# A fourth buffer for the weight sums of a fast matrix product, with tables loaded per mixer to make the room

## Chip, cores and metric

One core of a Trainium2 chip. The metric is device microseconds from the kernel's start to its end. TensorE (PE in the profile) multiplies, VectorE (DVE) and ScalarE (ACT) do the elementwise work, GpSimd (POOL) only issues transfers that add to what lies in the destination, SyncE (SP) issues most loads.

## The reference

An encoder of two layers on 512 tokens and 16 prepended ones, width 1024, all in float32:

```python
for l in range(DEPTH):                       # DEPTH = 2
    h = h + 0.5 * swiglu(rmsnorm(h, g[l, 0]), gate[l, 0], up[l, 0], down[l, 0])   # width 2816
    h = h + mixer(rmsnorm(h, g[l, 1]), ...)  # gated linear attention + softmax attention, merged by gates
    h = h + 0.5 * swiglu(rmsnorm(h, g[l, 2]), gate[l, 1], up[l, 1], down[l, 1])
return rmsnorm(h, final_norm)[:, N_META:]

def swiglu(x, w_gate, w_up, w_down):
    return (jax.nn.silu(x @ w_gate) * (x @ w_up)) @ w_down
```

In the softmax attention the queries and keys are turned by rotary angles, with a table of cosines and one of sines over the tokens. In the gated linear attention the decay comes from a low-rank product, `lr @ gla_w2 + gla_b2`.

## The kernel before

Activations lie with the channels on the 128 partitions and the 528 tokens along the free axis. Every float32 product is made from three products of rounded parts: a weight block of 128 x 1024 is split into a high part (`whi`, a cast on ACT, L287) and a low part (`wlo`, a subtraction on DVE, L288), and TensorE multiplies high by high, high by low and low by high.

In a feed-forward block the gate and up products go by a scheme with seven instead of eight products of half-size blocks (Strassen's, in Winograd's form), per pair of column groups. There are eleven pairs, and four more such sets of products for most of the down product. The seven products of a pair are named "1" to "7". Products "1", "2" and "4" use blocks of the weights as they are (`DIRECT`); "7", "3", "6" and "5" use sums of blocks, which are made while they are loaded:

- third and fourth sum (`s3`, `s4`, products "7" and "3") live in the pool of long sums, tag `wsa`;
- second and first sum (`s2`, `s1`, products "6" and "5") live in the pool of short sums, tag `wsb`.

Both pools are opened in `block_pools` with three buffers each; blocks used as they are have three buffers of their own (`wraw`), and four buffers hold high and low parts. For pairs 0 and 1 `s3` and `s4` begin as a negated copy of a block on ACT (L203), to which POOL's queue adds by a transfer (L208). From pair 2 on `s3` is loaded by SP (L198) and DVE subtracts a block from it (L253); `s4` is a subtraction on DVE (L256). `s1` is always a load by SP and an addition by POOL's queue. `begin_sums` asks for the sums of a pair when the block of its product "1" is fetched, nine loads ahead of use.

In the very first block the order of the products is P0 "1" "2", P1 "1" "2", P0 "4", P1 "4", P0 "6" "5" "7" "3", P1 "6" "5", P2 "1", P1 "7", P2 "2", P1 "3", P2 "6" "5" and so on: one product (a tile) is 24 matmuls. The order within each engine's queue is set by a planner when the program is built: it takes an instruction when its inputs and its buffer are there by its own reckoning, in the order of the program where several are. On the chip each queue then runs in that fixed order.

Rotary tables, identity and other constants lie in one tile `ct`, loaded by `load_constants` behind the first silu of the first block (L395 to L398); only 128 columns of it come earlier, by SP. The low-rank weights (`w2t`) have one tile for the whole program. A mixer opens its own pools on the left of the memory, where the sums' pools and the pool `c` of the feed-forward block lay; the operands (`x` or `xc`) lie on the right.

Of the kernel before, what the change touches and what calls it, by code (L numbers as in the profile page):

```python
# [10 lines left out]
F32 = mybir.dt.float32  # L11
F32R = mybir.dt.float32r
# [5 lines left out]
P = 128  # L18
D = 1024
KC = D // P  # L20
SEQ = 512
META = 16
T = SEQ + META
# [137 lines left out]
NPAR = G_FIN + KC  # L161


C_COS, C_SIN = 0, T
C_ID = 2 * T
C_O1024, C_O128, C_B64 = C_ID + P, C_ID + 2 * P, C_ID + 3 * P
C_DIAG = C_ID + 4 * P
NCONST = C_DIAG + P


class Weights:
# [157 lines left out]
def build(tc, ctx, xt, wts, win, par, w2, const, umask, out):  # L329
# [32 lines left out]
    def nm(p):  # L362
        count[0] += 1
        return f"{p}{count[0]}"
# [3 lines left out]
    def slot(tag, dtype=F32, n=None):  # L368
        return slots[tag].tile([P, T], dtype, tag=tag, name=nm(tag))[:, : n or live[0]]
# [24 lines left out]
    S.dma_start(pt, par)  # L394
    def load_constants():  # L395
        S.dma_start(ct[:, :C_O1024], const[:, :C_O1024])
        S.dma_start(ct[:, C_O1024 + P :], const[:, C_O1024 + P :])
        S.dma_start(mask, umask)  # L398

    eps = one.tile([P, 1], F32, name="eps")  # L400
    V.memset(eps, EPS)
    cos, sin = ct[:, C_COS : C_COS + T], ct[:, C_SIN : C_SIN + T]
    ident = ct[:, C_ID : C_ID + P]
    o1024, o128 = ct[:, C_O1024 : C_O1024 + P], ct[:, C_O128 : C_O128 + P]
    b64, diag2 = ct[:, C_B64 : C_B64 + P], ct[:, C_DIAG : C_DIAG + P]
# [384 lines left out]
    def gla_pair(l, p, lr, w2t, sr, qa, ka, va, n_out):  # L790
# [17 lines left out]
        for d in range(2):  # L808
            z = pair()
            for i, hs in enumerate(halves):  # L810
                c0 = p * 256 + d * P
                TE.matmul(z[:, i, :HF], w2t[:, c0 : c0 + P], lr[:, hs], start=True, stop=True)
            a, g, c, ct_ = slot("t"), slot("t"), slot("t"), slot("t")

            S.activation(v2(a), z[:, :, :HF], AF.Abs)
            S.activation(a, a, AF.Exp, scale=-1.0)
            S.activation(a, a, AF.Ln, bias=1.0)
            V.scalar_tensor_tensor(v2(g), z[:, :, :HF], 0.0, v2(a), ALU.min, ALU.subtract)
            ones = ct[:, C_COS + SEQ : C_COS + SEQ + 1]
            for bs in [b[1] for b in blocks] + [MB]:  # L820
                n = bs.stop - bs.start
                V.tensor_tensor_scan(c[:, bs], ones.broadcast_to([P, n]), g[:, bs], 0.0, ALU.mult, ALU.add)
            mid = blk(c)[:, :, 63:64].broadcast_to([P, NB, P])
            tot = blk(c)[:, :, 127:128].broadcast_to([P, NB, P])
            mm_ = c[:, T - 1 : T].broadcast_to([P, META])
            r16 = 1.0 / 16.0
            src = c
            if d == 1:
                V.tensor_tensor(g, c, g, ALU.subtract)
                src = g  # L830

            def to_end():
                V.tensor_tensor(blk(ct_), blk(src), tot, ALU.subtract)
                V.tensor_tensor(ct_[:, MB], src[:, MB], mm_, ALU.subtract)


            ke = slot("p")
            if d == 0:
                to_end()
                S.activation(ke, ct_, AF.Exp, scale=-r16)  # L840
            else:
                S.activation(ke, g, AF.Exp, scale=r16)
            V.tensor_tensor(ke, ka, ke, ALU.mult)
# [12 lines left out]
            V.tensor_tensor(blk(a), blk(src), mid, ALU.subtract)  # L856
            V.tensor_tensor(a[:, MB], src[:, MB], mm_, ALU.subtract)
            qp, kp = slot("p"), slot("p")
            S.activation(g, a, AF.Exp, scale=-r16)
            S.activation(a, a, AF.Exp, scale=r16)  # L860
            if d == 0:
                S.activation(c, c, AF.Exp, scale=r16)
                ein, eq, ek = c, a, g
            else:
                S.activation(ct_, ct_, AF.Exp, scale=-r16)
                ein, eq, ek = ct_, g, a
            V.tensor_tensor(qp[:, :n_out], qa, eq[:, :n_out], ALU.mult)
            V.tensor_tensor(kp, ka, ek, ALU.mult)
            if qin is None:
                qin = [slot("p"), slot("p")]  # L870
            e0 = 127 if d == 0 else 0
            for hh in range(2):
                rows = slice(hh * HD, (hh + 1) * HD)
                to = slice(d * HD, (d + 1) * HD)
                V.tensor_tensor(qin[hh][to, :n_out], qa[rows], ein[rows, :n_out], ALU.mult)
                V.tensor_copy(dec[to, hh, :], blk(ein)[rows, :, e0])
            prods.append((qp, kp))
# [70 lines left out]

    swap = [(i + 16) % 32 for i in range(32)]

    def rope(src, gc):

        n = src.shape[-1]
        sh = slot("t", n=n)
        V.stream_shuffle(sh, src, swap)
        V.scalar_tensor_tensor(src, src, col(gc), cos[:, :n], ALU.mult, ALU.mult)
        V.scalar_tensor_tensor(sh, sh, col(gc + 1), sin[:, :n], ALU.mult, ALU.mult)
        V.tensor_tensor(src, src, sh, ALU.add)

    def attention(l, x, rs, n_out):  # L960

        meta = n_out == T
        kt = project(x, rs, "i")
# [1 line left out]
        sq, y = slot("t"), slot("t")  # L965
        S.activation(sq, kt, AF.Square)
        rsqrt_of(means(b64, sq), y, True)
        rope(kt, G_KN + 2 * l)
        V.scalar_tensor_tensor(kt, kt, -0.5, y, ALU.mult, ALU.mult)

        vpp = pair()
# [24 lines left out]
        def prologue(g):  # L996
# [28 lines left out]
                    V.tensor_scalar(r, r, -0.0625, None, ALU.mult)  # L1025
            for c in range(2):
                q = qt[2 * g + c]
                rope(q, G_QN + 2 * l)
                if meta:
                    V.tensor_tensor(q[:, MB], q[:, MB], rq[:, 16 + c * META : 16 + (c + 1) * META], ALU.mult)  # L1030
                bt[2 * g + c] = slot("e", n=n_out)
                for e in range(2):
                    a, b = slice(e * HD, (e + 1) * HD), slice((1 - e) * HD, (2 - e) * HD)
                    qq = slot("p", F32R, n_out)
                    S.copy(qq[a], q[a])
                    V.tensor_tensor(qq[b], q[a], qq[a].bitcast(F32), ALU.subtract)
                    if meta:
                        V.tensor_copy(qm[:, 2 * c + e], qq[:, MB].bitcast(F32))
                    qs.append(qq)
# [82 lines left out]
        norm.pools = open_pools("right", **{"x": dict(x=16), "xc": dict(xc=8)}[kind])  # L1122

    def block_pools():
        pools = open_pools("left", wsa=3, wsb=3)
        W.long, W.short = pools["wsa"], pools["wsb"]
        return pools

    def mixer(l, norm, done, following):

        x, n_out = norm.x, T if l < DEPTH - 1 else SEQ
        pools = open_pools("left", e=8, i=5, p=7, q=6, k=5, lr=1)
        banks = open_pools("left", psum=("mm", "sm"), mm=2, sm=2)
        w2r, w2t, w2l = slots["p"].tile([P, T], F32, tag="p", name=nm("w2")), one.tile([P, 512], F32R, tag="w2", name=nm("w2")), slot("t")
        S.dma_start(w2r[:, :512], w2[l])
        w2r, w2l = w2r[:, :512], w2l[:, :512]
        S.copy(w2t, w2r)
        V.tensor_tensor(w2l, w2r, w2t.bitcast(F32), ALU.subtract)
# [10 lines left out]
            sr.append(r)  # L1149
        table("natural_log_exp_and_others")  # L1150
        lr = slot("lr", F32R)
        S.copy(lr[96:P], cos[96:P, SEQ : SEQ + 1].broadcast_to([32, T]))

        ps, both = Acc("sm"), slot("p", F32R)[:, : KC * HD].rearrange("p (k s m) -> p k s m", k=KC, s=2)
        for i, (copy, t) in enumerate(zip((S.copy, V.tensor_copy), W.row("w_in", KC))):
# [24 lines left out]
                gates.extend(project(x, None, both[:, i], n=n_out) for i in range(2))  # L1180

        gate_pairs(EARLY // 2)
        bt = attention(l, x, rs, n_out)
        gate_pairs(KC - EARLY // 2)
        live[0] = n_out
        a = [split(t, "x") for t in sr]
# [116 lines left out]
def constants():  # L1303
    f32 = np.float32
    inv = (f32(10000.0) ** (-np.arange(0, HD // 2, 2, dtype=f32) / f32(HD // 2))).astype(f32)
    row = np.repeat(np.arange(SEQ // 64), 64).astype(f32)
    colm = np.tile(np.arange(64), SEQ // 64).astype(f32)
    ang = np.zeros((HD, T), f32)
    sign = np.ones((HD, 1), f32)
    for d in range(HD):  # L1310
        ang[d, :SEQ] = (row if d < 32 else colm) * inv[d % 16]
        sign[d] = -1.0 if d % 32 < 16 else 1.0
    c = np.zeros((P, NCONST), f32)
    c[:, C_COS : C_COS + T] = np.tile(np.cos(ang), (2, 1))
    c[:, C_SIN : C_SIN + T] = np.tile(np.sin(ang) * sign, (2, 1))
    c[:, C_ID : C_ID + P] = np.eye(P)
    c[:, C_O1024 : C_O1024 + P] = 1.0 / D
    c[:, C_O128 : C_O128 + P] = 1.0 / P
    c[:, C_B64 : C_B64 + P] = np.kron(np.eye(2), np.ones((HD, HD))) / HD
    c[:, C_DIAG : C_DIAG + P] = 1.0 + np.eye(P)  # L1320
    return c, (np.arange(P)[:, None] > np.arange(P)[None, :]).astype(np.uint32)
# [49 lines left out]
```

## Time and profile before

| | us |
|---|---|
| median of 3 runs (lowest, highest) | 2209.68 (2209.25, 2211.64) |
| profiled execution, device time | 2211.05 |
| its span, first to last instruction | 2209.2 |
| PE, DVE, ACT, POOL busy | 2162.4, 1785.4, 1214.1, 101.8 |
| granted TensorE clock, mean | 0.997 |

In the rows below, L198 is a line of the kernel; `w<-win` is what is written and what it is made from, by the program's names with numbers left out; xN is a count. A row of the timeline is start, duration, engine, line, operation, and in brackets the idle time of the engine just before it and what ended that. A row of the stage table has, per engine, the busy time and the number of instructions, then the granted clock, the mean busy share of the 16 DMA engines and what they moved. The spans of DMA issues (SPq, POOLq) are those of the issuing queue; the transfer itself takes longer.

### The profile page before, as it was taken

The numbers are of one execution on the slowest core, as the hardware profiler recorded it, in microseconds if no ns is written. First come the engines' busy times: TensorE is split into PE (matmuls) and PEld (weight loads), VectorE is DVE, ScalarE is ACT, GpSimd is POOL, SyncE is SP. The second block draws the span as 40 slices with busy tenths as digits, with TensorE's granted clock in tenths as the row PEclk, the third lists the DMA queues.
The fourth block names the chain that finished last, engine by engine and source line by source line (L and its number), as shares of the span: only waits on it lengthen the run. The fifth ranks groups of instructions, "written<-read, shape, count | busy, mean of one in ns | idle before, by whom it ended". The sixth has DMA issues, their size and how long they took to land.

```text
span 2209.2 us, 40079 instructions
## 1 busy us (share of the span) xinstructions
PE 2162.4 (98%) x16506; PEld 2070.2 (94%) x16506; DVE 1785.4 (81%) x2703; ACT 1214.1 (55%) x1779; POOL 101.8 (5%) x120
## 2 busy tenths in 40 slices
PE   7999999999999999999999999999999999999998
PEld 6999999989999999999999999999788888999997
DVE  7897978486886689889789979775879767997987
ACT  7544545344785555454575445453457836554543
POOL 1000000000000001000010000000000001000100
PEclk9999999999999999999999999999999999999999
DMA  9775753212113468666567757432121145776752
GB/s 268 189 204 160 191 152 106 82 49 68 49 39 122 114 167 205 190 182 187 162 163 186 207 164 191 143 110 77 49 84 51 42 133 152 198 202 181 189 165 67
DMA packets 87463, 311.41 MB, mean 141 GB/s; under 512 B 9712, under 2 KB 12144, under 8 KB 87280
## 3 DMA queue, kind: packets, MB, share of 16 engines
q1 hardware_dynamic: 68624, 245.53, 32.9%
q0 software_dynamic: 16704, 60.82, 15.8%
q8 instruction: 130, 2.13, 0.4%
q10 hardware_dynamic: 1952, 2.50, 0.4%
q14 instruction: 53, 0.43, 0.1%
HBM read 289.94 MB, written 2.10 MB: 132 GB/s over the span
## 4 chain that ended last, share of the span: by engine, by line
PE 81%; DVE 11%; ACT 4%; issue 2%; DMA 2%; SPq 0%; DVEq 0%; ACTq 0%
PE ss L598 37%; PE mm L465 13%; PE ss L712 11%; PE ss L465 10%; PE sm L465 2%; DVE wlo L288 2%; DMA w<-win 2%; PE sm L1074 1%; PE ss L1049 1%; DVE g L678 1%; ACT whi L287 1%; PE sm L1090 1%; DVE h L720 1%; PE ss L471 1%; PE sm L1091 1%
## 5 line engine op out<-in xcount | busy, mean ns | idle before, releaser
L598 PE MATMUL ss<-xc,whi 128*128 128x264 f32 (+1 forms) x4928 | 907.2, 285 | 15.5 <-ACT whi L287 7.4
L598 PEld LDWEIGHTS ss<-xc,whi 128*128 128x128 f32 x4928 | 767.2, 189 | 20.4 <-ACT c L602 8.4
L598 PE MATMUL ss<-xc,wlo 128*128 128x264 f32 (+1 forms) x2464 | 702.5, 285 | 8.8 <-DVE wlo L288 8.8
L598 PEld LDWEIGHTS ss<-xc,wlo 128*128 128x128 f32 x2464 | 466.5, 189 | 11.1 <-DVE wlo L288 10.9
L288 DVE TENSOR_TENSOR wlo<-w,whi 128x1024 fp32r<-128x1024 f32 (+1 forms) x337 | 408.1, 1217 | 63.4 <-ACT whi L287 63.2
L287 ACT CAST whi<-w 128x1024 fp32r<-128x1024 f32 (+1 forms) x337 | 350.0, 1050 | 163.3 <-PE ss L598 80.5
L465 PE MATMUL mm<-x,whi 128*128 128x264 f32 (+1 forms) x1712 | 384.6, 315 | 0.0
L465 PEld LDWEIGHTS mm<-x,whi 128*128 128x128 f32 x1712 | 278.3, 188 | 16.5 <-issue 1.0
L465 PE MATMUL mm<-x,wlo 128*128 128x264 f32 (+1 forms) x856 | 266.0, 315 | 0.0
L712 PE MATMUL ss<-g,whi 128*128 128x264 f32 (+1 forms) x1280 | 237.4, 284 | 0.0
L287 ACT CAST whi<-raw 128x1024 fp32r<-128x1024 f32 x126 | 132.3, 1050 | 163.4 <-PE mm L465 102.3
L602 ACT COPY c<-ss 128x528 f32<-128x528 f32 (+1 forms) x132 | 78.5, 594 | 258.6 <-PE ss L598 258.6
L288 DVE TENSOR_TENSOR wlo<-raw,whi 128x1024 fp32r<-128x1024 f32 x126 | 153.9, 1222 | 59.0 <-ACT whi L287 58.1
L712 PEld LDWEIGHTS ss<-g,whi 128*128 128x128 f32 x1280 | 198.4, 188 | 0.1
L712 PE MATMUL ss<-g,wlo 128*128 128x264 f32 (+1 forms) x640 | 181.3, 283 | 0.0
L465 PEld LDWEIGHTS mm<-x,wlo 128*128 128x128 f32 x856 | 159.6, 188 | 8.5 <-issue 0.7
L465 PE MATMUL ss<-g,whi 128*128 128x264 f32 (+2 forms) x900 | 166.3, 299 | 0.0
L465 PEld LDWEIGHTS ss<-g,whi 128*128 128x128 f32 x900 | 131.7, 188 | 5.3
L208 POOL DMA_DIRECT2D w<-win x60 | 52.7, 878 | 1574.7 <-DVE wlo L288 582.5
L712 PEld LDWEIGHTS ss<-g,wlo 128*128 128x128 f32 x640 | 120.5, 188 | 0.0
L444 ACT ACTIVATE c<-c 128x528 f32<-128x528 f32 (+1 forms) x88 | 56.6, 643 | 98.5 <-DVE c L642 98.4
L465 PE MATMUL ss<-g,wlo 128*128 128x264 f32 (+2 forms) x450 | 106.2, 300 | 0.0
(267 smaller groups left out, 3370.2 us busy)
## 6 DMA issues: line engine op xcount, KB each, us to landing
w<-win SPq DMA_DIRECT2D x335, 512.0 KB, 4.5
raw<-wts SPq DMA_DIRECT2D x126, 512.0 KB, 3.3
w<-win POOLq DMA_DIRECT2D x60, 512.0 KB, 7.4
s<-win POOLq DMA_DIRECT2D x24, 512.0 KB, 7.2
w<-s POOLq DMA_DIRECT2D x24, 512.0 KB, 5.6
s<-w POOLq DMA_DIRECT2D x8, 512.0 KB, 9.6
h<-xt SPq DMA_DIRECT2D x3, 528.0 KB, 6.8
out<-h ACTq DMA_DIRECT2D x4, 256.0 KB, 2.4
```

The lines of the kernel that those rows point to most:

```text
L208: self.nc.gpsimd.dma_start(t, src, accum_op=ALU.add)
L287: nc.scalar.copy(hi[:, cs], w[:, cs])
L288: nc.vector.tensor_tensor(lo[:, cs], w[:, cs], hi[:, cs].bitcast(F32), ALU.subtract)
L444: prev_act[0] = S.activation(*args, **kw).ins
L465: TE.matmul(acc.half[i][:width], lhs, rhs[:, acc.spans[i]], start=first, stop=last)
L471: TE.matmul(a, weights, x[:, hs], start=True, stop=True)
L598: TE.matmul(acc[:, j], a[:, j, k], b[:, at], start=bool(begin and k == 0 and i == 0), stop=k == len(x) - 1 and i == 2, skip_group_check=no ...
L602: W.behind = S.copy(part(st, q), acc).ins
L678: V.tensor_tensor(r[into][:, ks], r[a][:, ks], r[b][:, ks], ALU.subtract)
L712: TE.matmul(acc[:, j], a[:, j, k], xs[b][:, k], start=bool(begin and k == 0 and i == 0), stop=k == 3 and i == 2, skip_group_check=not begin)
L720: V.tensor_tensor(to, to, acc, ALU.add)
L1049: TE.matmul(s[:n, i, :HF], lhs, kh[:, hs], start=True, stop=False)
```

## The change

Both pools of weight sums get a fourth buffer of 128 x 1024 float32. To make the room, the cosine and sine tables leave the tile of constants, and `w2t` leaves the pool of single tiles: each mixer opens a pool `cs` of three tiles, for `w2t` and the two tables, and loads the tables by POOL's queue. A tile of ones, `unit`, takes the place of a column of the cosine table that was used as ones.

```diff
...
-C_COS, C_SIN = 0, T
-C_ID = 2 * T
+C_ID = 0
...
+C_COS, C_SIN = NCONST, NCONST + T
...
         S.dma_start(ct[:, :C_O1024], const[:, :C_O1024])
-        S.dma_start(ct[:, C_O1024 + P :], const[:, C_O1024 + P :])
+        S.dma_start(ct[:, C_O1024 + P :], const[:, C_O1024 + P : NCONST])
...
-    cos, sin = ct[:, C_COS : C_COS + T], ct[:, C_SIN : C_SIN + T]
+    unit = one.tile([P, 1], F32, name="unit")
+    V.memset(unit, 1.0)
...
-            ones = ct[:, C_COS + SEQ : C_COS + SEQ + 1]
+            ones = unit
...
-    def rope(src, gc):
+    def rope(src, gc, angles):
         n = src.shape[-1]
+        cos, sin = angles
...
     def block_pools():
-        pools = open_pools("left", wsa=3, wsb=3)
+        pools = open_pools("left", wsa=4, wsb=4)
...
-        pools = open_pools("left", e=8, i=5, p=7, q=6, k=5, lr=1)
+        pools = open_pools("left", e=8, i=5, p=7, q=6, k=5, lr=1, cs=3)
...
-        w2r, w2t, w2l = slots["p"].tile([P, T], ...), one.tile([P, 512], F32R, tag="w2", ...), slot("t")
+        w2r, w2t, w2l = slots["p"].tile([P, T], ...), slot("cs", F32R)[:, :512], slot("t")
         S.dma_start(w2r[:, :512], w2[l])
+        angles = [slot("cs"), slot("cs")]
+        for t, c in zip(angles, (C_COS, C_SIN)):
+            G.dma_start(t, const[:, c : c + T])
...
-        S.copy(lr[96:P], cos[96:P, SEQ : SEQ + 1].broadcast_to([32, T]))
+        S.copy(lr[96:P], unit[96:P].broadcast_to([32, T]))
...
-        bt = attention(l, x, rs, n_out)
+        bt = attention(l, x, rs, n_out, angles)
...
-    c = np.zeros((P, NCONST), f32)
+    c = np.zeros((P, NCONST + 2 * T), f32)
```

More of the change, by code (lines that the diff above doesn't have):

```diff
@@ L958, in rope, with attention @@
         V.tensor_tensor(src, src, sh, ALU.add)
[L960 removed]
+    def attention(l, x, rs, n_out, angles):
         meta = n_out == T
@@ L967, in attention @@
         rsqrt_of(means(b64, sq), y, True)
-        rope(kt, G_KN + 2 * l)
+        rope(kt, G_KN + 2 * l, angles)
         V.scalar_tensor_tensor(kt, kt, -0.5, y, ALU.mult, ALU.mult)
@@ L1027, in prologue @@
                 q = qt[2 * g + c]
-                rope(q, G_QN + 2 * l)
+                rope(q, G_QN + 2 * l, angles)
                 if meta:
@@ L1131, in mixer @@
         x, n_out = norm.x, T if l < DEPTH - 1 else SEQ
-        pools = open_pools("left", e=8, i=5, p=7, q=6, k=5, lr=1)
+        pools = open_pools("left", e=8, i=5, p=7, q=6, k=5, lr=1, cs=3)
         banks = open_pools("left", psum=("mm", "sm"), mm=2, sm=2)
-        w2r, w2t, w2l = slots["p"].tile([P, T], F32, tag="p", name=nm("w2")), one.tile([P, 512], F32R, tag="w2", name=nm("w2")), slot("t")
+        w2r, w2t, w2l = slots["p"].tile([P, T], F32, tag="p", name=nm("w2")), slot("cs", F32R)[:, :512], slot("t")
         S.dma_start(w2r[:, :512], w2[l])
+        angles = [slot("cs"), slot("cs")]
+        for t, c in zip(angles, (C_COS, C_SIN)):
+            G.dma_start(t, const[:, c : c + T])
         w2r, w2l = w2r[:, :512], w2l[:, :512]
```

## The prediction

> **What bounds the kernel now.** I read the page first, then a table of busy time by stage.
>
> ```profile
> span 2209.2 us, 40079 instructions
> PE 2162.4 (98%) x16506; PEld 2070.2 (94%) x16506; DVE 1785.4 (81%) x2703; ACT 1214.1 (55%) x1779; POOL 101.8 (5%) x120
> ```
> ```profile
> core 0: us, PE busy (x) PEld busy (x) DVE busy (x) ACT busy (x) POOL busy (x), PEclk, DMA share, GB/s
> 0.00:70.00 70.00, 51.27 (x347) 47.95 (x348) 50.61 (x80) 49.50 (x75) 8.26 (x13) 0.98 0.87 256
> 70.00:340.00 270.00, 268.10 (x2174) 266.62 (x2173) 233.74 (x280) 136.72 (x161) 17.44 (x20) 0.99 0.63 174
> 404.00:700.00 296.00, 292.39 (x2344) 279.52 (x2343) 222.24 (x503) 180.25 (x367) 0.00 (x0) 1.00 0.19 62
> 775.00:1110.00 335.00, 331.99 (x2700) 329.99 (x2699) 281.35 (x345) 176.23 (x213) 22.71 (x26) 1.00 0.66 182
> ```
>
> TensorE is idle 2209.2 - 2162.4 = 46.8 us in all, and 70.0 - 51.3 = 18.7 us of that lies in the first 70 us. Later stages lack 2 to 4 us each. So buffers can buy something only in the opening; elsewhere they prefetch for an engine that is not waiting. The list of who waited for whom, for PE, over the whole span and then from 70 us on, says how much of the idle time belongs to weights:
>
> ```profile
> PE ss L598 <- DVE wlo L288: 8.8, 8, 3.1
> PE ss L598 <- ACT whi L287: 7.4, 1, 7.4
> PE ss L471 <- ACT whi L287: 1.6, 1, 1.6
> ```
> ```profile
> PE ss L471 <- DVE t L503: 1.1, 1, 1.1
> PE ss L598 <- DVE wlo L288: 1.0, 2, 0.6
> ```
>
> The 7.4 us are the start-up to the first weight. What is left is mostly two holes, both waits for the low half of a weight (L288), in the timeline of PE:
>
> ```profile
> 53.58 0.59 PE L598 MATMUL ss<-xc,wlo 128*128 128x264 f32 x1 [3.15 <-DVE wlo L288]
> 69.34 0.39 PE L598 MATMUL ss<-xc,wlo 128*128 128x264 f32 x1 [2.36 <-DVE wlo L288]
> ```
>
> Each is followed by a stretch at half clock (stage table, narrow windows):
>
> ```profile
> 53.40:56.80 3.40, 3.22 (x14) 3.23 (x15) 3.40 (x5) 0.65 (x1) 0.04 (x1) 0.50 0.86 290
> 70.50:73.90 3.40, 3.40 (x17) 3.27 (x15) 3.40 (x5) 0.44 (x1) 0.00 (x0) 0.50 0.15 37
> 74.00:77.40 3.40, 3.40 (x29) 3.40 (x29) 3.40 (x6) 1.15 (x2) 0.00 (x0) 1.00 0.78 248
> ```
>
> Half clock for 3.4 us costs 3.4 / 2 = 1.7 us (by the counts 17 against 29, 1.4). So the holes cost 3.15 + 1.7 = 4.85 and 2.36 + 1.7 = 4.06 us, together 8.9. The TensorE waits of 1.6 and 1.1 us show no such stretch beside them. The Trainium skill, page "TensorE: Matmul & The Clock Gate", section "HAM oscillation — how this bites in real kernels", gives the practical rule "no PE-idle gaps >~3.4µs"; by it neither hole would cost clock and closing the second would return 2.4 us instead of 4.1. The granted clock above, 0.50 behind a hole of 2.36 us, speaks against that limit here.
>
> Why the holes are there is in the timelines of DVE and of SP's queue:
>
> ```profile
> 35.53 1.22 DVE L288 TENSOR_TENSOR wlo<-s,whi 128x1024 fp32r<-128x1024 f32 x1
> 40.47 1.22 DVE L288 TENSOR_TENSOR wlo<-s,whi 128x1024 fp32r<-128x1024 f32 x1
> 45.28 1.22 DVE L288 TENSOR_TENSOR wlo<-w,whi 128x1024 fp32r<-128x1024 f32 x1
> 50.54 1.23 DVE L253 TENSOR_TENSOR w<-w,w 128x1024 f32<-128x1024 f32 x1 [3.42 <-DMA w<-win]
> 52.30 1.22 DVE L288 TENSOR_TENSOR wlo<-w,whi 128x1024 fp32r<-128x1024 f32 x1
> 55.80 1.22 DVE L288 TENSOR_TENSOR wlo<-s,whi 128x1024 fp32r<-128x1024 f32 x1
> 66.24 1.23 DVE L253 TENSOR_TENSOR w<-w,w 128x1024 f32<-128x1024 f32 x1 [4.92 <-DMA w<-win]
> ```
> ```profile
> 41.72 0.33 SPq L198 DMA_DIRECT2D w<-win  x1
> 57.05 0.33 SPq L198 DMA_DIRECT2D w<-win  x1
> ```
>
> L253 subtracts a block from the long sum of pair 2 (50.54) and of pair 3 (66.24). It stands in DVE's queue ahead of a split (L288) that TensorE needs, and it waits for the load of that long sum. Those loads go out at 41.72 and 57.05, right behind the ends of the splits of 40.47 and 55.80: they waited for a long buffer, which the split frees. The splits written wlo<-s are, in order, the third and fourth sums of pair 0 (35.53, 40.47) and the third of pair 1 (55.80).
>
> **The change part by part.**
>
> Long buffers, 3 to 4. With four, the pair 2 load no longer takes the second freed buffer but the first: 35.53 + 1.22 = 36.75 instead of 41.7, 4.9 us sooner. The pair 3 load takes the second instead of the third: 41.7 instead of 57.05, 15.3 us sooner. The copy of pair 1's fourth sum (L203) no longer waits for a buffer either, so the raw buffer that it reads comes free sooner:
>
> ```profile
> 37.04 1.05 ACT L203 ACTIVATE s<-w 128x1024 f32<-128x1024 f32 x1
> 28.99 2.00 ACT L287 CAST whi<-w 128x1024 fp32r<-128x1024 f32 x2 [1.32 <-DMA w<-win]
> ```
>
> Moved ahead, that copy fits into ACT's idle 1.32 us before 28.99; if it doesn't, up to 1.05 us go into the chain of squares and into TensorE's 1.6 us wait.
>
> Short buffers, 3 to 4. The second short sum of pair 1 (a load and an accumulating DMA on POOL's queue) need not wait for a release any more, and that of pair 2 has an earlier one to wait for. What that is worth hangs on the DMA engines (stage table):
>
> ```profile
> 15.00:20.00 5.00, 4.81 (x23) 4.32 (x22) 3.86 (x8) 3.83 (x8) 1.24 (x2) 1.00 1.02 343
> 25.00:30.00 5.00, 4.24 (x33) 3.82 (x32) 3.64 (x5) 3.68 (x6) 1.79 (x2) 1.00 1.06 260
> 45.00:50.00 5.00, 5.00 (x43) 5.00 (x42) 2.12 (x3) 2.04 (x3) 0.00 (x0) 1.00 1.00 253
> 66.00:72.00 6.00, 3.64 (x25) 3.43 (x24) 5.76 (x7) 2.49 (x3) 0.00 (x0) 0.87 0.00 0
> ```
>
> They are full up to 50 us and idle around the second hole. A block of 0.524 MB takes 0.524 / 0.343 = 1.5 us of full engines; an accumulation 0.524 / 0.253 = 2.1 us (estimates from these rows).
>
> First hole. The pair 2 load goes out 4.9 us sooner, but behind one more block (1.5 us) and perhaps an accumulation (2.1), so it lands 1.3 to 3.4 us before 50.5, at 47 to 49. Its L253 will also be placed sooner, since it follows its load in the planner's order: ahead of the split at 45.28 rather than behind it. DVE then stands still until 47 to 49 with one more needed split behind it, so the hole begins one tile earlier and ends about where it does. A tile's 24 matmuls take 2.9 us in the chain of waits:
>
> ```profile
> 901.12 2.92 PE ss L598 x24
> ```
> I take 0; bounds -4.85 (hole and clock go) and +2.9 (the blocked tile comes in addition).
>
> Second hole. The load has from 41.7 to 61.3 (66.24 - 4.92) to land; the engines have idle time from 50 on. I take the whole 2.36 + 1.7 = -4.06; bounds -4.06 and 0.
>
> Tables out of the opening. L396 loads 592 KB in the middle of the second load's flight:
>
> ```profile
> const<-const ACTq DMA_DIRECT2D x1, 592.0 KB, 6.9
> w<-win POOLq DMA_DIRECT2D x60, 512.0 KB, 7.4
> ```
>
> Of these, 2 x 128 x 528 x 4 bytes = 528 KB leave, 1.6 us of full engines; that helps the same hole, so I count nothing more.
>
> Tables and low-rank weights per mixer. Four loads of 264 KB on POOL's queue, in stages where POOL runs nothing (x0 above) and the DMA share is 0.19. Nothing queues behind them on POOL until the next block's sums. First use:
>
> ```profile
> L956 DVE SCALAR_TENSOR_TENSOR i<-i,par,const x10: 731/756/765, 526.4 to 1670.6; 128x528 f32<-128x528 f32 x6, 128x512 f32<-128x512 f32 x4
> ```
>
> The first use, at 526.4, lies 122 us into the stage that the table begins at 404, against 7.4 us for a landing: 0. Were the cover gone, 7 to 10 us per mixer would stand in rope. The low-rank weights only change place. One memset more on DVE while it waits for its first input: 0.
>
> Other block openings. The waits from 70 us on that buffers could touch are 1.0 + 1.1 us. I take -0.5; bounds -2.1 and +1 for a new order of the work.
>
> Sum: 0 - 4.06 + 0 - 0.5 = -4.6. The profiled execution took 2211.05 us (span 2209.2 and 1.85 around it), so 2206.5 on that scale; the median of the runs is 1.37 us lower, 2209.68, which gives 2205.1.
>
> **Rivals.**
>
> Both holes close: the pair 2 load lands by 44, or its L253 keeps its place behind the split. Then 2209.7 - 4.85 - 4.06 - 0.5 = 2200.3. For it: 4.9 us of lead against a DVE wait of 3.42. Against it: the full engines. Chance 0.17.
>
> The engines are the bound and nothing moves: earlier issue only lengthens the queue, and a hole of the second's size appears at another tile; or the three raw buffers, which stay, hold SP's queue instead, so that the change doesn't do what it says. Then 2209.7 - 0.5 = 2209.2. For it: share 1.00 and more for 45 us. Against it: 0.00 at 66 to 72. The Trainium skill, page "DMA: Bandwidth & Descriptors", section "Issuing engines are not separate DMA queues", has all issuers' transfers interleave on the same 16 engines, which is this rival's rule; the shares above agree with it for the first hole and not for the second. Chance 0.23.
>
> Slower. SP's queue stood still here, waiting for a raw buffer:
>
> ```profile
> 9.92 0.33 SPq L1286 DMA_DIRECT2D const<-const  x1
> 16.66 0.33 SPq L198 DMA_DIRECT2D w<-win  x1
> ```
>
> The second short sum of pair 1, not needed before the hole at 50.4, now fits in between, and gets ahead of the blocks for the fourth products, which were late already (the cast at 28.99 waited 1.32 us for one). ACT works in order, so a late cast holds the casts and squares behind it. The price is 1.5 + 2.1 = 3.6 us of engine time in front, a hole of that size near 32 us, and its half clock, 1.7: 2209.7 + 3.6 + 1.7 - 0.5 = 2214.5, if the later holes stay. It decides from about 3 us of delay on; TensorE has some tiles in hand before that. Chance 0.22.
>
> **How the numbers follow.** My forecast, 2205.1, has 0.38. A difference of 0.2%, 4.4 us, is about what a measurement of this kernel can tell from no change; the forecast lies just beyond it, so of its 0.38 I give 0.28 to faster and 0.10 to the same. With the rivals: faster 0.28 + 0.17 = 0.45, same 0.10 + 0.23 = 0.33, slower 0.22. The forecast's own range is 2202.5 (the first hole's -2 in addition) to 2208 (its +2.9). The range for 8 in 10 is 2200 to 2214.3: it takes in the case of both holes and ends just short of the slower one's middle.
>
> **What would show it.** Right: no TensorE wait of over 1 us between 57 and 75, granted clock 1.00 throughout 60 to 75, L253 of pair 3 without a DMA wait, the 592 KB issue gone, four POOL loads of 264 KB that nobody waits for. Wrong, if TensorE waits near 30 us for a cast that waits for a DMA, if the first hole vanishes with the second, or if a TensorE wait of over 1 us shows up in a mixer.

## The result, and the profile after

The changed kernel is slower: a median of 2216.7 us in 14 runs (2214.3 to 2219.56) against 2210.83 in 14 runs of the kernel before (2208.11 to 2215.65). The ratio is 1.0025, 95% interval 1.0017 to 1.0033, that is 5.9 us, outside the predicted range. The profiled execution took 2214.3 us, 3.3 over that of before; it is the shortest of its 14, so a part of the 5.9 us lies in stretches that differ from run to run and that one profile can't show. The mean granted clock was 0.997 in that execution and 0.996 in 10 of the 14; 0.001 of 2216 us is 2.2 us, so one or two more stretches at half clock in a usual run would be most of the difference (an estimate; no trace shows where they lie).

The page and the stage table, answering to the rows of before:

```profile
span 2212.5 us, 40074 instructions
PE 2163.5 (98%) x16506; PEld 2070.4 (94%) x16506; DVE 1782.7 (81%) x2704; ACT 1213.0 (55%) x1779; POOL 104.1 (5%) x124
```
```profile
0.00:70.00 70.00, 52.41 (x337) 48.90 (x338) 52.55 (x83) 47.12 (x72) 9.19 (x14) 0.95 0.94 270
70.00:340.00 270.00, 266.13 (x2163) 264.01 (x2162) 229.92 (x275) 137.30 (x162) 16.60 (x19) 1.00 0.61 168
404.00:700.00 296.00, 292.61 (x2342) 279.61 (x2341) 220.77 (x500) 181.40 (x368) 0.00 (x0) 1.00 0.18 60
51.10:54.50 3.40, 3.40 (x18) 3.40 (x17) 0.90 (x2) 0.00 (x0) 0.00 (x0) 0.50 0.99 228
57.90:61.30 3.40, 3.40 (x18) 3.40 (x17) 3.40 (x5) 0.85 (x2) 0.00 (x0) 0.50 0.72 210
```

The opening has not become shorter: 337 matmuls in the first 70 us where 347 were. The two stretches at half clock are still there, 2 and 13 us earlier. The second stage has 2.0 us less of TensorE's busy time than before. The opening's holes in the timeline of PE, and what DVE did:

```profile
50.75 0.39 PE L599 MATMUL ss<-xc,wlo 128*128 128x264 f32 x1 [2.36 <-DVE wlo L288]
55.80 0.60 PE L599 MATMUL ss<-xc,whi 128*128 128x264 f32 x3 [0.58 <-DVE rs L556]
57.46 0.39 PE L599 MATMUL ss<-xc,wlo 128*128 128x264 f32 x1 [1.06 <-DVE wlo L288]
```
```profile
36.78 1.22 DVE L288 TENSOR_TENSOR wlo<-s,whi 128x1024 fp32r<-128x1024 f32 x1
45.45 1.22 DVE L253 TENSOR_TENSOR w<-w,w 128x1024 f32<-128x1024 f32 x1 [4.39 <-DMA w<-win]
46.59 1.22 DVE L288 TENSOR_TENSOR wlo<-s,whi 128x1024 fp32r<-128x1024 f32 x1
49.48 1.22 DVE L288 TENSOR_TENSOR wlo<-w,whi 128x1024 fp32r<-128x1024 f32 x1
53.81 1.22 DVE L253 TENSOR_TENSOR w<-w,w 128x1024 f32<-128x1024 f32 x1 [2.50 <-DMA w<-win]
56.19 1.22 DVE L288 TENSOR_TENSOR wlo<-w,whi 128x1024 fp32r<-128x1024 f32 x1
```

The loads of both long sums did come sooner (L253 begins at 45.45 and 53.81 instead of 50.54 and 66.24). But both L253 also moved forward in DVE's queue, past two and three splits that stood ahead of them, and DVE stands 4.39 and 2.50 us at them. TensorE's holes come earlier, the first by one tile, the second by 11 us; they don't go away. The two loads go out at 38.03 and 47.84, each at the end of the split that frees its buffer (36.78 and 46.59), and the second of these splits stood behind the first L253.

The loss in the second stage is a place that had no hole before:

```profile
121.00 0.86 PE L713 MATMUL ss<-g,whi 128*128 128x264 f32 x2 [1.35 <-ACT g L674]
```
```profile
112.25 1.06 ACT L203 ACTIVATE s<-w 128x1024 f32<-128x1024 f32 x1 [3.17 <-DMA w<-win]
120.54 0.41 ACT L674 CAST g<-g 128x264 fp32r<-128x264 f32 x1 [0.83 <-DVE g L653]
```
```profile
104.91 0.87 POOL L208 DMA_DIRECT2D w<-win  x1 [6.85 <-DVE g L679]
113.71 0.87 POOL L208 DMA_DIRECT2D s<-win  x1 [7.93 <-ACT s L203]
```

Counted by the starts of the same matmuls in both traces, 2.3 of the 3.3 us of this profile are lost here, between TensorE's 701st and 751st matmul, and 1.6 more near 1158 us, where the third feed-forward block opens. The place is the end of the first group of pairs, where the sets of products for the down product begin (quads, from here on). ACT negates a raw block (L203) and waits 3.17 us for its load; what ACT does for the operands `g` comes 3 us late behind it, and TensorE misses one. POOL had begun a short sum's accumulation (104.91, landed at 112.02) just before SP issued the load of that block (105.49), and the block landed at 112.23: 6.7 us, against 4.3 before, where that accumulation, by its place in POOL's order, came at 117.75.

The tables did what the change says, and nobody waits for them:

```profile
cs<-const POOLq DMA_DIRECT2D x4, 264.0 KB, 4.3
```

### The profile page after: what moved, and what is told of

The parts are those of the page before. It is cut to its first block, busy times and chain, and to the rows that moved or that the text cites. A ratio compares the mean times of both kernels' runs of the same rounds, so it can differ in the third digit from the quotient of the medians.

```text
span 2212.5 us, 40074 instructions
## 1 busy us (share of the span) xinstructions
PE 2163.5 (98%) x16506; PEld 2070.4 (94%) x16506; DVE 1782.7 (81%) x2704; ACT 1213.0 (55%) x1779; POOL 104.1 (5%) x124
## 4 chain that ended last, share of the span: by engine, by line
PE 76%; DVE 14%; ACT 4%; DMA 3%; issue 3%; DVEq 0%; SPq 0%; ACTq 0%
PE ss L599 32%; PE mm L466 13%; PE ss L713 11%; PE ss L466 10%; DVE wlo L288 3%; DMA w<-win 3%; PE sm L466 2%; PE sm L1076 1%; PE ss L1051 1%; DVE g L679 1%; DVE h L721 1%; PE sm L1092 1%; ACT whi L287 1%; DVE c L675 1%; PE ss L472 1%
```

## The experiments

Two numbers from each trace sort the runs below: the start of TensorE's 401st matmul ("opening"; 78.2 us before, 78.0 after) and the time from there to its last one ("rest"; 2121.9 before, 2125.5 after). The rest counts all four feed-forward blocks' quads. They come from one profiled execution each; the times are medians of all runs, their ratio is to the kernel before on the same chip. One execution can have a stretch of half clock, worth up to 1.7 us, that another lacks, so a difference of under 2 us between two openings says little.

### One part of the change at a time

Tables and low-rank weights per mixer, three buffers of each kind:

```diff
-        pools = open_pools("left", wsa=4, wsb=4)
+        pools = open_pools("left", wsa=3, wsb=3)
```

> The tables and low-rank weights are loaded per mixer as in the changed kernel, but both sums' pools keep three buffers. Theory (the loss is in the orders that the fourth buffers give the queues): -2 to +1 us against the kernel before, both opening holes where they were before, the second one shorter (2.4 us down to 0 to 1.5) because the 592 KB load beside it is now 64 KB, no hole near 120 us. Rival (the loads per mixer and the moved memory cost the time): +3 to +6 us, found in the mixers.

Only the long pool with four:

```diff
-        pools = open_pools("left", wsa=4, wsb=4)
+        pools = open_pools("left", wsa=4, wsb=3)
```

> Four long buffers, three short ones, tables per mixer. Theory: the subtractions L253 of pairs 2 and 3 stand as early on DVE as in the changed kernel, wait 3 to 5 us and 2 to 3 us for their loads there, and PE has its holes near 48 and 55 us; no hole near 120 us; 0 to +2 us in all. Rival (the short buffers alone do the harm): the opening is as with three and three buffers, -2 to +1 us.

Only the short pool with four:

```diff
-        pools = open_pools("left", wsa=4, wsb=4)
+        pools = open_pools("left", wsa=3, wsb=4)
```

> Three long buffers, four short ones, tables per mixer. Theory: POOL's accumulation for the second quad's short sum again runs beside the load of that quad's first block, so ACT waits about 3 us for the block near 110 us and PE about 1.3 us near 120 us; in the opening L253 keeps its place of before; +2 to +4 us in all. Rival (the long buffers alone do the harm): no wait near 110 us, -2 to +1 us.

The changed kernel, with the long sum (L253) held on DVE behind the split that precedes it in the program:

```diff
-                nc.vector.tensor_tensor(lo[:, cs], w[:, cs], hi[:, cs].bitcast(F32), ALU.subtract)
+                self.split = nc.vector.tensor_tensor(lo[:, cs], w[:, cs], hi[:, cs].bitcast(F32), ALU.subtract).ins
...
-                V.tensor_tensor(got[f, i, "7"], got[f, i, "7"], self.kept1, ALU.subtract)
+                with self.tc.issue_after(self.split):
+                    V.tensor_tensor(got[f, i, "7"], got[f, i, "7"], self.kept1, ALU.subtract)
```

> The changed kernel, with L253 held behind the split of its own product's block on DVE, which is its place in the program. Theory (an early L253 stands before splits that PE needs): DVE no longer waits for a DMA at L253 in the opening, the holes near 48 and 55 us and their half clock go, 5 to 8 us less than the changed kernel, so 0 to -3 us against the kernel before; the hole near 120 us stays. Rival (the DMA engines are too slow for the opening in any order): holes of the same size at other tiles, within 2 us of the changed kernel.

| kernel | long/short buffers | median us | ratio, 95% interval | opening | rest |
|---|---|---|---|---|---|
| tables alone | 3/3 | 2205.89 | 0.9978 (0.9969, 0.9987) | 70.7 | 2121.6 |
| long four | 4/3 | 2216.2 | 1.0026 (1.0017, 1.0035) | 80.4 | 2125.2 |
| short four | 3/4 | 2220.23 | 1.0044 (1.0030, 1.0058) | 71.2 | 2138.5 |
| changed, long sum held | 4/4 | 2211.93 | 1.0004 (0.9995, 1.0012) | 72.2 | 2128.1 |

The tables' move, priced at nothing, is a gain of 4.7 us; the buffers, expected to bring 4.1, cost about 10.8 on top of it. All four runs missed what was expected of their time, the last by a little: -4.7 us against the kernel before where -2 to +1 was expected, +5.6 where 0 to +2 was, +9.7 where +2 to +4 was, and 4.8 us under the changed kernel where 5 to 8 was. The buffers cost in two places. The fourth long buffer costs the opening (70.7 to 80.4). The fourth short buffer costs the rest, 16.9 us over the tables alone. The list of waits of the kernel with four short buffers says how, and one place of it shows the pattern of the others:

```profile
ACT s L203 <- DMA w<-win: 23.6, 10, 4.8
PE ss L713 <- ACT g L674: 9.2, 7, 2.6
```
```profile
860.80 1.06 ACT L203 ACTIVATE s<-w 128x1024 f32<-128x1024 f32 x1 [2.83 <-DMA w<-win]
869.09 0.41 ACT L674 CAST g<-g 128x264 fp32r<-128x264 f32 x1 [0.83 <-DVE g L653]
```
```profile
869.56 0.86 PE L713 MATMUL ss<-g,whi 128*128 128x264 f32 x2 [0.94 <-ACT g L674]
```

With the tables alone the same ACT row reads 2.3 us in four waits, and PE has no wait for `g`. Holding the long sum took the opening of the changed kernel from 78.0 to 72.2 us and its time down by 4.8 us (ratio of the medians 0.998), which makes DVE's order the cause of the holes there; the rest did not get shorter (2128.1 against 2125.5).

### The tables' place, and the orders with three and with four

Tables in fixed memory, loaded once, by POOL's queue at the first mixer:

```diff
+    angles = [one.tile([P, T], F32, name=n) for n in ("cos", "sin")]
...
-        angles = [slot("cs"), slot("cs")]
-        for t, c in zip(angles, (C_COS, C_SIN)):
-            G.dma_start(t, const[:, c : c + T])
+        if l == 0:
+            with tc.issue_after(W.added):
+                for t, c in zip(angles, (C_COS, C_SIN)):
+                    G.dma_start(t, const[:, c : c + T])
```

> Three buffers of each kind, as before; the rotary tables stay in fixed memory as before and w2 too, but the tables are loaded once, on POOL's queue at the first mixer, not with the constants in the opening. Theory (540 KB less in the transfer that ran in the opening is what closes the second hole and shortens the first): as with the tables alone per mixer, 4 to 5.5 us under before (2205 to 2207), no half clock near 53 and 70 us. Rival (the gain came from the per-mixer buffers, that is from where things lie and the order the planner then finds): 2209.5 to 2211.5.

Tables alone, and the long sum held as above:

> Three buffers, tables per mixer, and the long sum of pairs 2 to 10 held on DVE behind the split that stands ahead of it in the program. Theory (what is left of the two holes, 0.74 and 0.50 us, is DVE standing at these sums): 0.5 to 1.2 us under the tables alone, about 2205. Rival (the sums are now late for the short sums built on them, so another wait opens): 1 to 3 us over the tables alone, 2207 to 2209.

Four short buffers; for pairs and quads the first short sum is asked for behind the second raw block, for the quads its accumulation goes behind the other short sum's:

```diff
     def first_sum(self, f, i):
-        s1 = self.block(f, i, "21", self.short, "wsb")
-        self.add(s1, self.dram(f, i, "22"))
+        with self.tc.issue_after(self.loaded):
+            s1 = self.block(f, i, "21", self.short, "wsb")
+        if i < NPAIR:
+            self.add(s1, self.dram(f, i, "22"))
...
+                with self.tc.issue_after(self.quad_added):
+                    self.add(got[f, i, "5"], self.dram(f, i, "22"))
```

> Three long and four short buffers, tables per mixer, and the first short sum's load held on SP behind the load of the second raw block, its accumulation for the quads held on POOL behind the accumulation into the other short sum. Theory (the fourth short buffer cost 14 us because these transfers went ahead of the raw block, so that ACT stood 23.6 us in ten waits at its negation, with the copy of PE's operand behind it): 10 to 14 us less than with the four short buffers alone, 2205.5 to 2210; ACT's waits at the negation under 5 us in all, PE's waits for g under 3 us. Rival (a fourth buffer lets the transfers pile up on the 16 engines whatever their order): under 5 us back, 2215 to 2220.

Both holds in the changed kernel:

> The changed kernel, four of each, with both orders written out: the long sum behind the split, the short sum behind the second raw block and the other accumulation. Theory (the buffers themselves cost nothing, only the orders that they let the planner choose; what is left is the gain of the tables): 2204.5 to 2207.5, 4 to 7 us under the changed kernel with the long sum held alone. Rival (four buffers cost by themselves): 2210 to 2213, no difference to the changed kernel with the long sum held alone.

| kernel | long/short | median us | ratio, 95% interval | opening | rest |
|---|---|---|---|---|---|
| tables late, once | 3/3 | 2206.73 | 0.9978 (0.9968, 0.9987) | 75.8 | 2119.7 |
| tables alone, long sum held | 3/3 | 2202.85 | 0.9963 (0.9950, 0.9976) | 70.4 | 2121.6 |
| short four, short sums held | 3/4 | 2212.95 | 1.0012 (1.0003, 1.0020) | 72.7 | 2130.4 |
| changed, both held | 4/4 | 2225.09 | 1.0066 (1.0053, 1.0079) | 72.1 | 2143.1 |

The gain of the tables is that they leave the opening; per mixer or once makes no difference. It was not as sure as expected at the second hole, which stood with 2.85 us at 67.4 in that profile, half clock behind it; what went for certain is the first. The second goes with a race that the record shows: where it stood (the kernel before, this one, and below the tables alone without an accumulation), POOL's accumulation went out 0.02 to 0.29 us ahead of the load of pair 3's long sum, which took 8.4 to 9.2 us; in the profile of the tables alone that load went out 0.44 us ahead and took 6.1. The long sum held gives 3.0 us more, where 0.5 to 1.2 was expected from a profile in which the second hole happened to be closed. The hold of the short sums failed in an instructive way. With four short buffers it gave back half, 7.3 us where 10 to 14 was expected, and left a loss of over 1 us at only one of the quads' places. But ACT's waits at the negation only fell from 23.6 to 17.1 us: the hold put another accumulation, the one before it in POOL's order, beside the raw block (at the first place, issued at 95.0 us, with the block at 98.5 taking 5.7). With four of each it made things 13 us worse, in part since it also moved the pairs' short sums: at 1125 us one of their accumulations now ran beside the blocks that open the next feed-forward block, and with the pairs left alone (next section) about 8 of the 13 us come back.

### Narrower holds, and the hold on the kernel before

Long four, short three, long sum held:

> Four long and three short buffers, tables per mixer, the long sum held on DVE behind the split ahead of it. Theory (the fourth long buffer cost 10 us only by letting the planner put this sum ahead of splits that PE waits for): 8 to 13 us under the same without the hold (2216.2), so 2203 to 2208, near the same hold with three buffers (2202.9). Rival (the earlier load of the long sum's buffer costs by itself, by sharing the 16 engines with the raw blocks): 2210 to 2214, the holes back at other tiles.

Short four, the hold of the short sums for the quads only (`i >= NPAIR`):

> Three long and four short buffers, tables per mixer; only for the quads the first short sum's load is held on SP behind the second raw block and its accumulation on POOL behind the accumulation into the other short sum, the pairs as the planner has them. Theory (the loss of four short buffers lies at the quads' ends, and the losses of the wider hold at its openings come from the pairs that it displaced): 2206 to 2211, 2 to 7 us under the wider hold. Rival (four short buffers crowd the engines in any order): 2212 to 2220.

The changed kernel with the long sum held and the quads' hold:

> The changed kernel with the long sum held behind the split and the quads' first short sum held as in the run beside it. Theory (only the orders cost): 2203.5 to 2209. Rival (with four of each, the extra transfers in flight delay whatever block stands next, in another place for each order): 2211 to 2220.

The kernel before, tables in the opening, with the long sum held:

> The kernel before, tables still loaded in the opening, with the long sum held behind the split ahead of it. If both holes are DVE standing at this sum: the holes shrink below 1 us and the half clock after them goes, 7 to 9 us under before, 2202 to 2204, as with the tables moved as well. If the second hole is the load of the constants itself, which delays the raw block: half of that, 2205.5 to 2208.

| kernel | long/short | median us | ratio, 95% interval | opening | rest |
|---|---|---|---|---|---|
| long four, long sum held | 4/3 | 2217.83 | 1.0032 (1.0022, 1.0042) | 79.1 | 2128.9 |
| short four, quads held | 3/4 | 2214.46 | 1.0014 (1.0004, 1.0024) | 71.8 | 2130.0 |
| changed, long sum and quads held | 4/4 | 2217.14 | 1.0034 (1.0022, 1.0047) | 72.1 | 2134.0 |
| before, long sum held | 3/3 | 2203.53 | 0.9966 (0.9953, 0.9978) | 71.8 | 2122.1 |

The last row is the clearest. One hold in the kernel before, with no buffer more, closes both holes and takes their half clock away, 7.7 us for the 8.9 that the prediction had counted. Its timelines of DVE and PE in the opening (lines are one further on):

```profile
53.70 1.22 DVE L289 TENSOR_TENSOR wlo<-s,whi 128x1024 fp32r<-128x1024 f32 x1
60.53 1.22 DVE L289 TENSOR_TENSOR wlo<-w,whi 128x1024 fp32r<-128x1024 f32 x1
61.66 1.23 DVE L254 TENSOR_TENSOR w<-w,w 128x1024 f32<-128x1024 f32 x1
62.80 1.23 DVE L289 TENSOR_TENSOR wlo<-s,whi 128x1024 fp32r<-128x1024 f32 x1
```
```profile
51.46 0.39 PE L599 MATMUL ss<-xc,wlo 128*128 128x264 f32 x1 [0.75 <-DVE wlo L289]
67.58 0.51 PE L599 MATMUL ss<-xc,whi 128*128 128x264 f32 x2 [0.77 <-DVE c L619]
```

The first long sum of this stretch stands at 61.66 and finds its block there. So the holes were never a lack of buffers. With the tables moved as well the gain is about the same (0.9963 against 0.9966): two cures for one loss.

The other three rows speak for the rival. With these orders written out four buffers still cost, in other places each time: the long four at 51 us, the others at the quads.

### The accumulation beside the raw block

On SP, the first raw block of pair 3 held behind the load of pair 1's first short sum, in the kernel with four long buffers and the long sum held:

```diff
+            late = (f, i, name, tag) == ((0, 0), 3, "11", "raw")
+            with self.tc.issue_after(self.first_load) if late else nullcontext():
+                self.loaded = self.nc.sync.dma_start(...).ins
```

> Four long and three short buffers, tables per mixer, the long sum held on DVE, and on SP the first raw block of pair 3 held behind the load of pair 1's first short sum, as three buffers have them. If the 7 to 8 us that this kernel lost in the opening without the second hold are this one item of SP's queue (its hole of 4.2 us at 51 us and the half clock after it): 6 to 8.5 us less, 2209 to 2212, no hole over 1.5 us in 44 to 60 us. If a longer queue of transfers delays whatever comes next there: less than 3 us back, 2215 or more.

The quads' accumulation left out, in the kernel with the tables alone, with four short buffers, and in the changed one with the long sum held (product 5 of the quads then gets one block in place of a sum of two, so these three measure the transfer and don't compute the encoder):

```diff
-        self.add(s1, self.dram(f, i, "22"))
+        if i < NPAIR:
+            self.add(s1, self.dram(f, i, "22"))
```

> Three buffers, tables per mixer; the quads' first short sum leaves out its accumulation (product 5 of the quads gets one block in place of a sum of two). The measure for the two runs beside it: 0 to 2 us under the tables alone (2205.9), by either theory, because ACT's and PE's waits on the quads are small there already.

> Four short buffers, tables per mixer, the same accumulation left out. If it is this transfer beside the raw block that costs: at most 4 us over the same with three buffers (14.3 us with the accumulations), ACT's waits at the negation under 6 us in all. If it is the order of the queues, or the earlier plain loads: 8 to 14 us over it.

> Four of each, long sum held, the same accumulation left out. If the accumulations beside the raw block are the whole of what four buffers cost with the long sum held: within 2 us of three buffers without them. If the earlier plain loads cost too: 4 to 8 us over those.

| kernel | long/short | median us | ratio, 95% interval | opening | rest |
|---|---|---|---|---|---|
| long four, long sum and SP's load held | 4/3 | 2218.14 | 1.0028 (1.0017, 1.0038) | 77.5 | 2128.7 |
| tables alone, without it | 3/3 | 2206.54 | 0.9974 (0.9962, 0.9985) | 74.7 | 2120.6 |
| short four, without it | 3/4 | 2205.25 | 0.9968 (0.9957, 0.9980) | 70.9 | 2123.6 |
| changed, long sum held, without it | 4/4 | 2203.32 | 0.9959 (0.9946, 0.9971) | 72.9 | 2119.9 |

Without this one transfer per quad the cost of the fourth short buffer is gone: in the rest 3.0 us where it was 16.9, and with four of each the rest is as short as with three. There, with both causes taken out, nothing is left of what four buffers cost: 0.9959 of before, against 0.9963 for three buffers with the long sum held. Three buffers gain nothing from its absence. ACT's row of waits at the negation reads, with four short buffers and without the accumulation:

```profile
ACT s L203 <- DMA w<-win: 3.4, 6, 1.4
```

3.4 us instead of 23.6, and no wait of PE for `g` is left in the list. So the loss at the quads is the accumulation that a free buffer lets start ahead of, and then run beside, the raw block that ACT waits for. Taking it out also frees its place in the queues, so the run doesn't part its bytes from its place; the wider hold, which changed the place alone, gave back 8.1 of the 16.9 us.

The SP run was a miss. Its opening stayed at 77.5 us, and the trace of the same kernel without that hold had held the reason all along, on another queue, beside the ACT cast that came late:

```profile
36.90 0.86 POOL L208 DMA_DIRECT2D w<-s  x1 [8.71 <-DMA s<-win]
46.57 0.86 POOL L208 DMA_DIRECT2D s<-w  x1 [8.80 <-DMA w<-s]
47.23 1.12 POOL L208 DMA_DIRECT2D w<-win  x1
```
```profile
54.39 1.99 ACT L288 CAST whi<-w 128x1024 fp32r<-128x1024 f32 x2 [5.81 <-DMA w<-win]
```

POOL's queue stood 8.80 us before the accumulation that ends pair 1's last long sum (s<-w), which can't begin until the one before it has landed; behind it stood the accumulation (w<-win) whose result ACT needs first. With three long buffers the w<-win is first of the two, at 39.03 us with the tables alone and the long sum held.

### The square of two orders

In the opening only, POOL's accumulation s<-w held behind that w<-win, in the kernel with four long buffers, without and with the hold on DVE:

```diff
+                with self.tc.issue_after(self.first_added) if (f, i) == ((0, 0), 1) else nullcontext():
                     self.add(s4, got[f, i, "6"])
```

> Four long and three short buffers, tables per mixer; in the opening, POOL's accumulation into the last long sum of pair 1 held behind the one into its first short sum, as three buffers have them; DVE's long sums left where the planner puts them, ahead of the splits. If POOL's order alone costs the opening: 5 to 9 us under the same without it (2216.2), so 2207 to 2211. If DVE's long sums cost it too, as in the changed kernel, where POOL's order is already this one: 2213 to 2218, holes of 2 us near 48 and 56 us as in the changed kernel.

> The same with the long sum held on DVE as well. If the two orders together are what the opening costs: 6 to 9 us under the same with the DVE hold alone (2217.8), so 2208.5 to 2212, no hole over 1.5 us in 44 to 60 us; what is left over three buffers with the hold (2202.9) lies at the quads, where ACT waits for raw blocks. If neither order but the earlier transfers cost it: less than 3 us back.

| four long, three short buffers | median us | ratio, 95% interval | opening | rest |
|---|---|---|---|---|
| neither held | 2216.2 | 1.0026 (1.0017, 1.0035) | 80.4 | 2125.2 |
| long sum on DVE held | 2217.83 | 1.0032 (1.0022, 1.0042) | 79.1 | 2128.9 |
| POOL's order held | 2211.18 | 1.0002 (0.9993, 1.0011) | 75.4 | 2122.9 |
| both | 2210.64 | 1.0001 (0.9992, 1.0009) | 71.5 | 2127.7 |

Both orders cost the opening of this kernel, and either hides behind the other: holding both takes 8.9 us off it, POOL's alone 5.0, DVE's alone 1.3, which is no more than one stretch of half clock. With POOL's alone TensorE still waits 2.93 us for a low half at 48 us. With both held the opening is within 1.1 us of that with three buffers. What it then loses, 6.1 us of the rest, is again at the quads: ACT's waits at the negation are 14.8 us there.

Of the kernels that compute the encoder two are the fastest, and the intervals don't part them: three buffers of each with the long sum held, with the tables per mixer (2202.85 us, 0.9963 of before, 0.9950 to 0.9976) or in the opening as before (0.9966). Both beat the kernel before and the changed one.

## Why the prediction was wrong, step by step

**Where the bound was: right.** The two holes and their half clock cost what they were said to cost. The kernel before with one hold got 7.7 of 8.9 us back.

**Why the holes were there: half right.** L253 waited for a load that waited for a buffer, and a split stood behind it: all three are in the trace. Only the last is what had to change. The prediction's cure was the buffer; the run that left the buffers alone and moved L253 closed both holes.

**First hole, 0: right, by its own reasoning.** L253 did move ahead of the split at 45.28 (and of one more), the hole did begin one tile earlier (48.39 instead of 50.43) and ended at 50.75 instead of 53.58, with its half clock.

**Second hole, -4.06: the step that failed.** The load had "from 41.7 to 61.3 to land", and it did, at 53.79. But both ends of that stretch were of the old order. It went out at 47.84, not 41.7: the split that frees its buffer stood behind the first L253, which waited 4.39 us for its own load. And 61.3 was L253's place before. The sentence used for the first hole, that L253 follows its load in the planner's order, holds for the second too, and was not applied: it was put at 53.81, three splits early, DVE stood 2.50 us, and TensorE's waits of 0.58 and 1.06 us were followed by half clock as the old hole was. In place of -4.06 for the second hole and 0 for the first, the opening came out at 78.0 us against 78.2.

**Tables out of the opening, nothing extra: wrong by 4.7 us.** They were said to help "the same hole", the second. Alone they take the first hole away (0.74 us or no row at all in its place; 0.95 in the profile without the quads' accumulation), and the second in one of these three profiles.

**"Elsewhere they prefetch for an engine that is not waiting", -0.5 with +1 as the worst: mis-sized, and for the wrong reason.** In the changed kernel's profile the rest grew by 3.6 us, with the long sum held by 6.2, with four short buffers alone by 16.6. TensorE was not waiting there because the transfers came in a good order; that the DMA share was 0.63 in the stage said nothing about the one block on which ACT stands.

**Rivals.** The slower one had the mechanism, a short sum's accumulation that gets ahead of a raw block, but set it at pair 1 of the opening, at 3.6 + 1.7 us. There it cost under 0.9 us (by the start of TensorE's 201st matmul): the block for the fourth product landed at 29.60 instead of 28.96 and the ACT cast waited 1.82 us instead of 1.32. Its real place is the end of the groups with quads, two in each of the four feed-forward blocks: with four short buffers alone ACT waits at all eight, in the changed kernel's profile at the first of them. That the engines are the bound and a hole appears at another tile came true in the opening, but at 2209.2 us this rival priced the new holes like the old and saw none in the rest. The rule quoted with it, that all issuers' transfers interleave on the same 16 engines (the Trainium skill, page "DMA: Bandwidth & Descriptors", section "Issuing engines are not separate DMA queues"), agrees with the block that took 6.7 instead of 4.3 us beside an accumulation.

**The signs that it named** answered plainly: clock 1.00 from 60 us on and L253 of pair 3 without a wait both failed, the 592 KB issue is gone and nobody waits for the POOL loads. Of the three signs of being wrong none came: between 28 and 39 us TensorE waited no longer than 0.53 us, the first hole didn't vanish, and no wait of over 1 us stood in a mixer. They watched for the rivals, and the forecast failed in a way that none of them named. One sum is off beside that: the forecast's 2205.1 with 2 us less is 2203.1, not 2202.5.

What stays open: why the transfers in flight at 41 to 51 us land sooner with the tables elsewhere, though the tables are only loaded after 53 us (pair 2's long sum: issued at 41.48, landed at 47.83, against 41.72 and 50.45); and where the 2.6 us lie by which the median of the changed kernel lies further from before than its profile.

## What to carry to other kernels

Where a planner sets the order of queues that run in order, one more buffer is an edit of that order: ask, for every operation that the buffer lets start sooner, what it is put in front of on its engine and on its DMA queue, and who stands behind. If a hole is an engine standing at a job that nobody needs yet, with a needed one behind it, move the job; here that took one hold in the program and was worth more than the memory. And look for the late transfer on every queue before holding one: the SP hold was spent on a wait that POOL's queue explained.

## What the hardware showed beyond that

The clock can be halved without an idle TensorE before it. In the kernel with the tables alone, in a mixer, TensorE had no gap of over 0.4 us from 545 us on, and yet (stage table):

```profile
562.00:565.40 3.40, 3.40 (x17) 3.33 (x17) 2.26 (x7) 1.68 (x4) 0.00 (x0) 0.52 0.01 2
```

The same with the long sum held, with 20 matmuls between 562.6 and 566.0; before and after have 30 there, at clock 1.00. What stands just ahead of it, from 558.7 to 562.1 us, are 29 matmuls, as many as elsewhere; but 16 of them write two columns each and 4 write 16, so that 2064 columns pass where 29 matmuls of 264 columns are 7656.

Two counts over the twenty traces of this case put this together with the holes. The granted clock changes only at whole multiples of 3.413 us from its first change. And cut at these points, from 20 to 2190 us, every one of the 19 pieces in which the matmuls that began in it had up to 2112 columns was followed by a piece at half clock; none with over 3200 was; in between both happen. So the length of a gap alone doesn't tell: 1.98 us at 39.4 us (tables late, once) was followed by half clock, 2.14 us at 38.9 us (tables alone, long sum held) was not. This is a count, not an experiment. A piece at half clock costs up to 1.7 us; those near 22 us, with four long buffers and the long sum held, cost 0.3 us or less by the start of TensorE's 201st matmul.

The Trainium skill, page "TensorE: Matmul & The Clock Gate", section "Part 1: The HAM clock gate (the "warmup" mystery)", has the clock set by a free-running window of activity, so that what happens depends on where in it an event falls; the steps of 3.413 us agree with that, and so do gaps that were followed by half clock in one trace and not in another.
